# A block with an MLP by Strassen: sums on VectorE, two weight sums kept in DRAM, four products in sequence

## The chip, the core and the metric

The program runs on one core of a Trainium2 chip. Times are device microseconds. The kernel before was timed three times: 778.31, 778.51 and 778.95 us. The change is timed against it on the same chip, and beside it stands one profiled execution of each kernel.

The core has a matrix engine (TensorE, PE in the profile, with its weight loads shown as PEld), VectorE (DVE), ScalarE (ACT), GpSimd (POOL) and SyncE (SP). SyncE issues most of the loads here; GpSimd's and ScalarE's queues issue some DMAs too. Each engine takes its own instructions in a fixed order and waits on semaphores for the others.

## The reference

One encoder block on 512 tokens of width 1024: two attention branches with gates, a norm, and then the part that is changed, a gated MLP and its norm.

```python
u, g = jnp.split(x @ w_ffn_in[layer], 2, axis=-1)          # 1024 -> 2 x 2816
h = jax.nn.gelu(causal_dwconv(u, conv_w[layer], conv_b[layer])) * g
x = layer_norm(DEEPNORM_ALPHA * x + h @ w_ffn_out[layer], ln2_g[layer], ln2_b[layer])
```

All is float32. The kernel writes each operand of a product as a high part in a shorter format (float32r) and a low part, and forms a product from three matmuls: high by high, high by low, low by high.

## The kernel before, in words

**The MLP's first product** runs over 22 blocks of 128 features (the index f). Each needs a piece of weights u_f and a piece g_f, and each piece feeds 24 matmuls over 8 chunks of 128 rows (function ffn_in, lines 701 to 707). `activate(f)` (from line 712) does the causal convolution, the GELU and the product with g: ScalarE copies u out of PSUM (L715), VectorE does three steps (L717 to L719), ScalarE the GELU (L720), VectorE the multiplication into `hp` (L724), which also frees g's PSUM bank.

**The MLP's second product** takes the features two blocks at a time: a pair i holds an even and an odd block, 11 pairs in all (NP). Tokens fall into two halves of 256, output columns into two halves of 512. On this two-by-two scheme Strassen's method needs seven products m1 to m7 where eight would be plain. Each of the seven costs, for one pair, 2 blocks of 128 tokens by 3 matmuls.

Three of the seven (m3, m4 and the part of m1 for that pair) are done inside the first stage, one pair after another (`second_half`, 18 matmuls a pair). Their weights come as two pieces p_i of 512 KB, which `mix_weights` (L752 to L754) turns into sums on GpSimd. Their activations come from `sides` (L726 to L747), which forms sums and differences of the four quarters of `hp` on GpSimd (L735, L738 to L740) and splits them on ScalarE and VectorE. `gh`, `gl` are used at once; `eh`, `el` are kept for all 11 pairs.

The other four products (m5, m7 added into m1, m2, and m6 added into m3; 66 matmuls each) form the second stage. Their weights are loaded again as 22 pieces: a_i holds both feature halves of the right output columns, b_i of the left ones; one GpSimd sum per piece (`mix_low` L760, `mix_top` L767), then the split. A piece a_i serves m5 and m7, b_i serves m2 and m6. The last five b pieces are held in SBUF (HELD), so that block 0 can be finished first, and then block 1: m2, then m6 in two halves of 256 columns.

**Loads and splits.** The class `Stream` (lines 53 to 111) has one list of pieces in order. When a piece is asked for (`get`), loads and splits are issued up to three pieces ahead. A raw piece lands in one of three buffers `raw` (in the second stage two more, `raw2`, for some pieces); ScalarE writes the high part (L94), VectorE the low part (L96; GpSimd for some early pieces), into a ring of three slots `whi`, `wlo` or where `place` names another home. A slot is free when the matmuls of its last piece are done. SyncE issues the loads in the order of the list and waits at each for its raw buffer.

**Order and memory.** The program is traced in the order of the code; a planner with a model of the engines' times then sets the order on each engine, and the semaphores follow. `tc.issue_after(x)` puts the instructions of its block behind x on their engine. The PSUM banks are two pools of four: `pa` holds m4, then m5 and m2, beside the u and g in work; `pb` holds m3 and m1, later the last half of m6. When the first stage is over its tiles are given up and the pool `wp` takes their place.

**The end.** `into` (L859 to L866) adds a product into the residual row tiles x1[j] on VectorE, `finish(j)` (L868 to L884) normalises a tile of 128 tokens and writes it out. Tiles 0 and 1 are finished while m2 and m6 run, tile 2 during block 1, tile 3 after the last matmul.

Of the kernel before, what the change touches and what calls it, by code (L numbers as in the profile page):

```python
# [24 lines left out]
NP = FC // 2  # L25
# [13 lines left out]
HELD = 5  # L39
# [13 lines left out]
class Stream:  # L53


    def __init__(self, nc, raw, ring, pieces, ahead_load, ahead_split, place=None, lo_on_pool=()):
# [5 lines left out]
        self.mixed, self.homes = {}, {}  # L62
        self.nl = self.ns = 0

    def _advance(self, upto):
        nc = self.nc
        n = len(self.pieces)
        while self.nl < min(n, upto + self.al):
            key, src = self.pieces[self.nl]
            srcs = src if isinstance(src, tuple) else (src,)  # L70
            ts = []
            for m, one in enumerate(srcs):
                t = self.home(key, m)
                w = int(np.prod(one.shape[1:]))
                dst = t[:, :w]
                nc.sync.dma_start(dst if len(one.shape) == 2 else dst.rearrange("p (a b) -> p a b", b=one.shape[-1]), one)
                ts.append(t)
            self.loaded[self.nl] = (ts, w)
            self.nl += 1
        while self.ns < min(n, upto + self.asp, self.nl):  # L80
            ts, w = self.loaded.pop(self.ns)
            key = self.pieces[self.ns][0]
            if key in self.mixed:
                parts = self.mixed[key](ts)
            else:
                parts = [(ts[0], w, key)]
            out = ()
            for t, w, where in parts:
                if where in self.place:
                    hi, lo = self.place[where](where)  # L90
                else:
                    hi = self.ring.tile([128, 1024], F32R, tag="whi", name=f"whi_{self.ns}")
                    lo = self.ring.tile([128, 1024], F32R, tag="wlo", name=f"wlo_{self.ns}")
# [5 lines left out]
            self.ns += 1  # L99

# [14 lines left out]
def tile_block(ctx: ExitStack, tc: tile.TileContext, xT, xN, w_qi, w_ki, w_t, w_v, w_br, w_o, w_fi, w_fo,  # L115
# [52 lines left out]
    low, top = ([(f"{key}{i}", w_fo[:, i, :, b * 512:b * 512 + 512].rearrange("d p n -> p d n")) for i in range(NP)]  # L168
                for b, key in ((1, "a"), (0, "b")))
# [7 lines left out]
    st = Stream(nc, rawp, ring, order, 3, 3, place, POOL_LO)  # L177

# [547 lines left out]
    def sides():  # L726
# [3 lines left out]
        sm = tp.tile([128, 5, HT], F32, tag="sm", bufs=1, name=f"sm{i}")  # L730
        gh = tp.tile([128, 3, HT], F32R, tag="gh", bufs=1, name=f"gh{i}")
        gl = tp.tile([128, 3, HT], F32R, tag="gl", bufs=1, name=f"gl{i}")
        nc.scalar.activation(gh[:, 0:2], hp[:, 1:3], AF.Copy)
        nc.vector.tensor_sub(gl[:, 0:2], hp[:, 1:3], r32(gh[:, 0:2]))
        nc.gpsimd.tensor_add(sm[:, 4], hp[:, 1], hp[:, 2])  # L735
        nc.scalar.activation(gh[:, 2], sm[:, 4], AF.Copy)
        nc.vector.tensor_sub(gl[:, 2], sm[:, 4], r32(gh[:, 2]))
        nc.gpsimd.tensor_add(sm[:, 0:2], hp[:, 0:2], hp[:, 2:4])  # L738
# [4 lines left out]
        nc.scalar.activation(a, sm[:, 0:4], AF.Copy)  # L743
        nc.vector.tensor_sub(b, sm[:, 0:4], r32(a))
# [3 lines left out]

    def mix_weights(ts):
# [3 lines left out]
        nc.gpsimd.tensor_sub(a[:, 1], a[:, 1], a[:, 0])  # L753
        nc.gpsimd.tensor_add(a[:, 0], a[:, 0], b[:, 1])  # L754
        return [(ts[1], 512, "pb"), (ts[0], 1024, "pa")]

    def mix_low(key):
        def f(ts):
            w = ts[0].rearrange("p (d n) -> p d n", d=2)
            nc.gpsimd.tensor_add(w[:, 0], w[:, 0], w[:, 1])  # L760
            return [(ts[0], 1024, key)]
        return f

    def mix_top(key):
        def f(ts):
            w = ts[0].rearrange("p (d n) -> p d n", d=2)
            nc.gpsimd.tensor_add(w[:, 1], w[:, 0], w[:, 1])  # L767
            return [(ts[0], 1024, key)]
# [5 lines left out]

    place["pb"] = place_low
    for i in range(NP):
        st.mixed[f"p{i}"] = mix_weights
        st.mixed[f"a{i}"] = mix_low(f"a{i}")
        st.mixed[f"b{i}"] = mix_top(f"b{i}")
# [27 lines left out]
    for f in range(FC):  # L807
        if f == 0:
            ups, gps_ = ps0[0], ps0[1]
        else:  # L810
# [5 lines left out]
            if f % 2 == 0:  # L816
# [3 lines left out]
                second_half(f // 2 - 1, h, st.get(f"p{f//2-1}"))  # L820
            gps_ = pa("g_ps")
# [6 lines left out]
    wa = []  # L828

    def fifth(i, blocks=(0, 1)):  # L830
        product(m5, (eh[i][:, 1], el[i][:, 1]), [w[:, second_c] for w in wa[i]], i == 0, i == NP - 1, blocks)

    def seventh(i):
        product(m1, (eh[i][:, 2], el[i][:, 2]), [w[:, first_c] for w in wa[i]], False, i == NP - 1)

    last = st.get(f"p{NP-1}")
    wa.append(st.get("a0"))
    fifth(0)
# [4 lines left out]
    def place_b(key):  # L843
        return (wp.tile([128, 1024], F32R, tag="dh", bufs=HELD, name=f"{key}h"),
                wp.tile([128, 1024], F32R, tag="dl", bufs=HELD, name=f"{key}l"))

    for key in ["a2", "a3", "a4"] + [f"b{i}" for i in range(NP - HELD, NP)]:
        place[key] = place_b

    def more_raw(key):  # L850
        return wp.tile([128, 1024], F32, tag="raw2", bufs=2, name=f"raw_{key}")

    for n, key in enumerate([f"a{i}" for i in range(2, NP)] + [f"b{i}" for i in range(NP)]):
        if n % 5 in (1, 3):
            st.homes[key, 0] = more_raw
# [31 lines left out]
    for i in (1, 2):  # L887
        wa.append(st.get(f"a{i}"))
        fifth(i)
    second_half(NP - 1, h, last)  # L890
    wa.append(st.get("a3"))
    fifth(3)
    for t in range(2):
        into(2 + t, second_c, m1[t], 1.0, first=True)
    for i in range(4):
# [129 lines left out]
```

## Time and profile before

| | us |
|---|---|
| median of three runs | 778.51 |
| the profiled execution | 783.59 |
| its span, first to last instruction | 781.8 |
| TensorE busy in it | 756.8 (97%) |
| VectorE busy | 561.6 (72%) |
| ScalarE busy | 355.9 (46%) |
| GpSimd busy | 251.2 (32%) |

The MLP's first product runs from about 414 us to 697.6, the second stage of the second product from there to 772.6, the last norm and output to 781.8. A group's row names line, engine, operation, output<-inputs, shapes and count, then busy us and mean ns, then the idle time before and who ended it. A row of waits gives total us, times and the longest. A row by stretch gives its length, then busy time and number of instructions of each engine, TensorE's granted clock (1.00 is full), the DMA engines' busy share and GB/s. A timeline row gives start and duration. Matmuls overlap in the pipeline: 0.39 us is the way through, and the step from one to the next is shorter.

### The profile page before, as it was taken

To read this page: it belongs to the slowest core of one execution; us is meant where nothing else is said; L and a number is where in the kernel's file an instruction comes from. 1 tells how busy PE (TensorE), PEld (TensorE's weight loads), DVE (VectorE), ACT (ScalarE), POOL (GpSimd) and SP (SyncE) were. 2 spreads that over 40 slices of the span, in tenths; PEclk is the share of its full clock that TensorE was granted. 3 is DMA by queue.
4 is the path that set the end of the run, shared out by engine and by line. 5 is a ranking of instruction groups with operands and counts; after the bars stand their busy time and mean duration, and the time that the engine had idled before them with its cause. 6 is when DMAs were issued, how large, how long until landed. Compare 5 with 4: busy or idle time off the path is not lost.

```text
span 781.8 us, 9787 instructions
## 1 busy us (share of the span) xinstructions
PE 756.8 (97%) x3579; PEld 630.7 (81%) x3579; DVE 561.6 (72%) x826; ACT 355.9 (46%) x550; POOL 251.2 (32%) x227
## 2 busy tenths in 40 slices
PE   8999999999999999999999999999999999988985
PEld 6788887788888888888889888888888888877864
DVE  5579999977666575658663766776676667776797
ACT  5546654656564746836211533433344334433340
POOL 2002534527814110000100442334233423466451
PEclk9999999999999999999999999999999999999998
DMA  7642332233324333126700443333334332438532
GB/s 241 222 157 81 108 108 68 68 109 83 106 95 121 95 106 97 54 81 224 288 0 1 135 137 130 109 133 122 126 107 135 132 120 98 132 111 257 174 119 97
DMA packets 32160, 95.55 MB, mean 122 GB/s; under 512 B 3880, under 2 KB 4280, under 8 KB 32112
## 3 DMA queue, kind: packets, MB, share of 16 engines
q1 hardware_dynamic: 27728, 84.19, 33.1%
q10 hardware_dynamic: 2576, 6.29, 3.0%
q0 software_dynamic: 1808, 4.44, 1.6%
q8 instruction: 28, 0.46, 0.2%
q14 instruction: 20, 0.16, 0.1%
HBM read 88.59 MB, written 4.21 MB: 119 GB/s over the span
## 4 chain that ended last, share of the span: by engine, by line
PE 68%; DVE 7%; issue 3%; POOL 2%; ACT 1%; DMA 1%; POOLq 0%; DVEq 0%; ACTq 0%
PE u_ps L706 5%; PE u_ps L707 5%; PE g_ps L706 5%; PE g_ps L707 5%; PE g_ps L705 5%; PE u_ps L705 5%; PE m_ps L786 3%; PE m_ps L787 3%; PE m_ps L788 3%; PE av_ps L404 2%; PE ga_ps L254 2%; PE ga_ps L253 2%; PE ga_ps L255 2%; PE o_ps L665 2%; PE o_ps L664 2%
## 5 line engine op out<-in xcount | busy, mean ns | idle before, releaser
L96 DVE TENSOR_TENSOR wlo<-raw,whi 128x1024 fp32r<-128x1024 f32 (+2 forms) x104 | 146.1, 1406 | 70.9 <-ACT whi L94 67.8
L94 ACT ACTIVATE whi<-raw 128x1024 fp32r<-128x1024 f32 (+2 forms) x123 | 126.2, 1027 | 110.7 <-issue 35.0
L705 PE MATMUL u_ps<-x1h,whi 128*128 128x512 f32 (+1 forms) x192 | 71.5, 373 | 0.2 <-ACT x1h L688 0.2
L706 PE MATMUL u_ps<-x1l,whi 128*128 128x512 f32 (+1 forms) x192 | 71.4, 372 | 0.1
L707 PE MATMUL u_ps<-x1h,wlo 128*128 128x512 f32 (+1 forms) x192 | 71.3, 372 | 0.0
L706 PE MATMUL g_ps<-x1l,whi 128*128 128x512 f32 (+1 forms) x184 | 69.9, 380 | 0.0
L705 PE MATMUL g_ps<-x1h,whi 128*128 128x512 f32 (+1 forms) x184 | 69.9, 380 | 0.0
L707 PE MATMUL g_ps<-x1h,wlo 128*128 128x512 f32 (+1 forms) x184 | 69.9, 380 | 0.0
L96 POOL TENSOR_TENSOR wlo<-raw,whi 128x1024 fp32r<-128x1024 f32 x19 | 46.2, 2435 | 18.6 <-ACT whi L94 18.5
L720 ACT ACTIVATE c<-c,cwt 128x512 f32<-128x512 f32 x22 | 15.9, 724 | 59.7 <-DVE c L719 59.7
L705 PEld LDWEIGHTS u_ps<-x1h,whi 128*128 128x128 f32 x192 | 36.2, 188 | 6.8 <-ACT x1h L688 0.5
L706 PEld LDWEIGHTS u_ps<-x1l,whi 128*128 128x128 f32 x192 | 36.2, 188 | 6.5 <-DVE x1l L689 0.3
L707 PEld LDWEIGHTS u_ps<-x1h,wlo 128*128 128x128 f32 x192 | 36.2, 188 | 6.2
L705 PEld LDWEIGHTS g_ps<-x1h,whi 128*128 128x128 f32 x184 | 34.6, 188 | 6.6
L707 PEld LDWEIGHTS g_ps<-x1h,wlo 128*128 128x128 f32 x184 | 34.6, 188 | 6.5
L706 PEld LDWEIGHTS g_ps<-x1l,whi 128*128 128x128 f32 x184 | 34.6, 188 | 6.5
L393 DVE TENSOR_TENSOR ptl<-tr_ps,pth 128x512 fp32r<-128x512 f32 (+1 forms) x48 | 27.4, 595 | 13.6 <-ACT pth L392 13.5
L445 POOL TENSOR_TENSOR beta<-beta,keep 128x1280 f32<-128x1280 f32 x8 | 20.6, 2570 | 48.6 <-DVE keep L444 43.2
L714 POOL MEMSET u<- 128x2 f32 x22 | 2.1, 99 | 89.5 <-DVE c L719 89.5
L622 POOL DMA_DIRECT2D ln<-in_lnp_dram x4 | 2.3, 573 | 82.6 <-PE ga_ps L255 82.6
L392 ACT ACTIVATE pth<-tr_ps 128x512 fp32r<-128x512 f32 (+1 forms) x48 | 23.5, 520 | 11.3 <-PE tr_ps L388 8.9
L724 DVE TENSOR_TENSOR hp<-g_ps,c 128x512 f32<-128x512 f32 x22 | 15.2, 690 | 18.1 <-PE g_ps L707 16.5
(563 smaller groups left out, 2095.9 us busy)
## 6 DMA issues: line engine op xcount, KB each, us to landing
raw<-in_w_fi_dram SPq DMA_DIRECT2D x44, 512.0 KB, 3.3
raw<-in_w_fo_dram SPq DMA_DIRECT2D x37, 512.0 KB, 3.4
raw<-in_w_t_dram SPq DMA_DIRECT2D x32, 512.0 KB, 3.4
raw<-in_w_v_dram SPq DMA_DIRECT2D x8, 512.0 KB, 4.3
raw<-in_w_br_dram SPq DMA_DIRECT2D x8, 512.0 KB, 3.3
raw<-in_w_o_dram SPq DMA_DIRECT2D x8, 512.0 KB, 4.1
xr<-in_xT_dram SPq DMA_DIRECT2D x8, 256.0 KB, 5.0
raw<-in_w_qi_dram SPq DMA_DIRECT2D x8, 256.0 KB, 4.2
```

The lines of the kernel that those rows point to most:

```text
L94: nc.scalar.activation(hi[:, :w], t[:, :w], AF.Copy)
L96: self.low = eng.tensor_sub(lo[:, :w], t[:, :w], r32(hi[:, :w])).ins
L392: nc.scalar.activation(th[:, :width], ps[:, :width], AF.Copy)
L393: lows = nc.vector.tensor_sub(tl[:, :width], ps[:, :width], r32(th[:, :width]))
L445: nc.gpsimd.tensor_mul(beta, beta, keep[:, 1:ATT + 1])
L705: nc.tensor.matmul(ps[:, c], wh[:, kc], x1h[:, k, c], start=(k == 0), stop=False)
L706: nc.tensor.matmul(ps[:, c], wh[:, kc], x1l[:, k, c], start=False, stop=False)
L707: nc.tensor.matmul(ps[:, c], wl[:, kc], x1h[:, k, c], start=False, stop=(k == KC - 1))
L720: nc.scalar.activation(c, c, AF.Gelu_apprx_tanh, bias=cwt[:, f, 3:4])
L786: nc.tensor.matmul(o, xh_[:, r], wh[:, c], start=start, stop=False, skip_group_check=True)
L787: nc.tensor.matmul(o, xh_[:, r], wl[:, c], start=False, stop=False, skip_group_check=True)
L788: mm = nc.tensor.matmul(o, xl_[:, r], wh[:, c], start=False, stop=stop, skip_group_check=True)
```

## The change

- **Sums on VectorE.** All sums of `sides` and `mix_weights` go from GpSimd to VectorE. Some are made in place in `hp`; the two sums that keep a tile of their own have one buffer `sm` between them. `eh`, `el` are split in two parts (three quarters, one quarter). p_i's second raw piece gets a buffer of its own (`rawb`).
- **Two weight sums kept.** After p_i a new piece s_i, without a load, calls `keep_sums`: from the mixed weights it forms the weights of m6 (split at once into high and low part) and of m7 (kept whole, float32) on VectorE and ScalarE, and GpSimd's queue writes the three 256 KB tiles to DRAM.
- **Four products in sequence.** The second stage's weights come in units of two pairs: v (six loads, raw right quarter, for m5), x (m7's sum from DRAM, split on chip), y (raw left quarter, m2), z (m6's high and low part from DRAM, straight to their place, no split). The order is m5, then the last pair's `second_half`, then m7, m2, m6. The buffers `raw2` and HELD are gone; six buffers of 8 KB per partition take the units that are not in the ring.
- **Order around it.** m5's first two units run block 0 and then block 1. The additions into x1 move to where their products end. g2 and b2 are loaded after m5. z's loads stand behind y's on SyncE's queue. m6's whole second block is done in halves of 256 columns.

```diff
+            if key in self.direct:
+                ts = self.tiles(key)
+                for t, one in zip(ts, src):
+                    w = int(np.prod(one.shape[1:]))
+                    nc.sync.dma_start(r32(t[:, :w]).rearrange("p (a b) -> p a b", b=512), one)
...
-            order.append((f"p{f//2-1}", (w_fo[0, f // 2 - 1], w_fo[1, f // 2 - 1])))
+            order += [(f"p{f//2-1}", (w_fo[0, f // 2 - 1], w_fo[1, f // 2 - 1])), (f"s{f//2-1}", ())]
...
-    order += low + top
+    order += raw_half("v", 1, slice(512, 1024))
+    order += [(f"x{u}", sums[u][2].rearrange("i p n -> p i n")) for u in range(NU)] + raw_half("y", 0, slice(0, 512))
+    kept = [(f"z{u}", [sums[u][n].rearrange("i p n -> p i n") for n in range(2)]) for u in range(NU)]
...
-        nc.gpsimd.tensor_add(sm[:, 4], hp[:, 1], hp[:, 2])
...
-        nc.gpsimd.tensor_add(sm[:, 0:2], hp[:, 0:2], hp[:, 2:4])
-        nc.gpsimd.tensor_sub(sm[:, 2], hp[:, 3], hp[:, 2])
-        nc.gpsimd.tensor_sub(sm[:, 3], hp[:, 0], hp[:, 1])
+        nc.vector.tensor_add(s1, hp[:, 1], hp[:, 2])
...
+        nc.vector.tensor_sub(s3, hp[:, 0], hp[:, 1])
+        nc.vector.tensor_add(hp[:, 0:2], hp[:, 0:2], hp[:, 2:4])
+        nc.vector.tensor_sub(hp[:, 2], hp[:, 3], hp[:, 2])
...
-        nc.gpsimd.tensor_sub(b[:, 0], b[:, 0], b[:, 1])
-        nc.gpsimd.tensor_sub(a[:, 1], a[:, 1], a[:, 0])
-        nc.gpsimd.tensor_add(a[:, 0], a[:, 0], b[:, 1])
+        nc.vector.tensor_sub(b[:, 0], b[:, 0], b[:, 1])
+        nc.vector.tensor_sub(a[:, 1], a[:, 1], a[:, 0])
+        nc.vector.tensor_add(a[:, 0], a[:, 0], b[:, 1])
...
+    def keep_sums(i):
+        def f(_):
+            a, b = (t.rearrange("p (k n) -> p k n", k=2) for t in mixing[i])
+            nc.vector.tensor_add(b[:, 0], b[:, 0], a[:, 0])
+            whole_ = tp.tile([128, 512], F32, tag="s7", bufs=1, name=f"s7_{i}")
+            nc.vector.tensor_add(whole_, a[:, 1], a[:, 0])
+            hi = tp.tile([128, 512], F32R, tag="sh", bufs=1, name=f"sh{i}")
+            lo = tp.tile([128, 512], F32R, tag="sl", bufs=1, name=f"sl{i}")
+            nc.scalar.activation(hi, b[:, 0], AF.Copy)
+            nc.vector.tensor_sub(lo, b[:, 0], r32(hi))
+            for n, half in enumerate((r32(hi), r32(lo), whole_)):
+                nc.gpsimd.dma_start(sums[i // 2][n, i % 2], half)
+            return []
...
+    def unit(pss, row, key, u, w, blocks=(0, 1), c=slice(0, 512), start=True):
+        for n in range(min(2, NP - 2 * u)):
+            i = 2 * u + n
+            part = [x[:, n * 512:n * 512 + 512] for x in w]
+            mm = product(pss, (eh[i][:, row], el[i][:, row]), part, start and i == 0, i == NP - 1, blocks, c)
+        return mm
...
+    v = [st.get("v0"), st.get("v1")]
+    for t in range(2):
+        for u in range(2):
+            unit(m5, 1, "v", u, v[u], (t,))
+    second_half(NP - 1, h, last)
...
+    for u in range(2, NU):
+        w = st.get(f"v{u}")
+        if firsts:
+            with tc.issue_after(st.low):
+                for _ in range(2):
+                    into(*firsts.pop(0), 1.0, first=True)
+        unit(m5, 1, "v", u, w)
+    g2, b2 = bcast(wp, 2), bcast(wp, 3)
+    held = []
+    for u in range(NU):
+        unit(m1, 2, "x", u, st.get(f"x{u}"), start=False)
+        if u == 0:
+            for t in range(2):
+                into(t, second_c, m5[t], 1.0, stats=1)
+                into(t, first_c, m5[t], -1.0)
+    for u in range(NU):
+        unit(m2, 0, "y", u, st.get(f"y{u}"))
+        with tc.issue_after(st.load):
+            held.append(zt.get(f"z{u}"))
+        if u < 2:
+            into(u, first_c, m1[u], 1.0, stats=0)
+            finish(u)
+    for u in range(NU):
+        mm = unit(m3, 3, "z", u, held[u], (0,), start=False)
...
+        for u in range(NU):
+            mm = unit(m3, 3, "z", u, held[u], (1,), lo_c, start=False)
+    into(3, slice(512, 768), m3[1][:, lo_c], 1.0, stats=1)
     with tc.issue_after(mm):
+        for u in range(NU):
+            unit(end, 3, "z", u, held[u], (1,), hi_c, start=True)
```

More of the change, by code (lines that the diff above doesn't have):

```diff
@@ L75, in _advance @@
                 dst = t[:, :w]
-                nc.sync.dma_start(dst if len(one.shape) == 2 else dst.rearrange("p (a b) -> p a b", b=one.shape[-1]), one)
+                self.load = nc.sync.dma_start(dst if len(one.shape) == 2 else dst.rearrange("p (a b) -> p a b", b=one.shape[-1]), one).ins
                 ts.append(t)
-            self.loaded[self.nl] = (ts, w)
+            self.loaded[self.nl] = (ts, w if ts else 0)
             self.nl += 1
@@ L88, in _advance @@
             for t, w, where in parts:
[L89 to L93, printed above, removed]
+                hi, lo = self.tiles(where)
                 nc.scalar.activation(hi[:, :w], t[:, :w], AF.Copy)
@@ L99, in _advance, with tiles @@
             self.ns += 1
+    def tiles(self, key):
+        if key in self.place:
+            return self.place[key](key)
+        return tuple(self.ring.tile([128, 1024], F32R, tag=f"w{n}", name=f"w{n}_{key}") for n in ("hi", "lo"))
     def home(self, key, m):
@@ L167, in tile_block @@
     order += [(f"wo{k}", w_o[k]) for k in range(KC)]
-    low, top = ([(f"{key}{i}", w_fo[:, i, :, b * 512:b * 512 + 512].rearrange("d p n -> p d n")) for i in range(NP)]
-                for b, key in ((1, "a"), (0, "b")))
+    sums = [nc.dram_tensor(f"s_sum{u}", (3, min(2, NP - 2 * u), 128, 512), F32, kind="Internal").ap() for u in range(NU)]
     for f in range(FC + 1):
@@ L841, in tile_block, with place_unit @@
     wc, wp = open_pool("wp", side="right", reuse_waits="tile")
[L843 to L855, printed above, removed]
+    def place_unit(key):
+        t = wp.tile([128, 2048], F32R, tag="d", bufs=6, name=f"d_{key}")
+        return t[:, :1024], t[:, 1024:]
+    for key in (f"{k}{u}" for k in "vxyz" for u in range(NU)):
+        if key not in RING_UNITS:
+            place[key] = place_unit
     parts2 = [padded(dp, [128, 3 if j == 3 else 2, 6], name=f"parts2_{j}") for j in range(NB)]
@@ L902, in tile_block @@
         if firsts:
             with tc.issue_after(st.low):
-                into(*firsts.pop(0), 1.0, first=True)
-        fifth(i)
-        seventh(i)
-    m2 = [pa(f"m2_ps{t}") for t in range(2)]
-    def second(i, w, blocks):
-        return product(m2, (eh[i][:, 0], el[i][:, 0]), [x[:, first_c] for x in w], i == 0, i == NP - 1, blocks)
-    def sixth(i, w, blocks, c=slice(0, 512), pss=m3, start=False):
-        return product(pss, (eh[i][:, 3], el[i][:, 3]), [x[:, second_c] for x in w], start, i == NP - 1, blocks, c)
@@ L916, in tile_block @@
-    for i in range(2):
-        w = st.get(f"b{i}")
-        second(i, w, (0, 1))
-        sixth(i, w, (0, 1))
-    for t in range(2):
-        into(t, second_c, m5[t], 1.0, stats=1)
-        into(t, first_c, m5[t], -1.0)
-        into(t, first_c, m1[t], 1.0, stats=0)
-    for i in range(2, NP - HELD):
-        w = st.get(f"b{i}")
-        second(i, w, (0, 1))
-        sixth(i, w, (0, 1))
-    held = [(i, st.get(f"b{i}")) for i in range(NP - HELD, NP)]
-    finish(0)
-    finish(1)
-    for i, w in held:
-        second(i, w, (0,))
-        mm = sixth(i, w, (0,))
@@ new lines, in tile_block @@
+    m2 = [pa(f"m2_ps{t}") for t in range(2)]
+    for u in range(NU):
[7 more added lines that the diff above has]
+        mm = unit(m3, 3, "z", u, held[u], (0,), start=False)
+        if u == 0:
+            for t in range(2):
+                into(2 + t, first_c, m2[t], 1.0, stats=0)
+                into(2 + t, second_c, m2[t], -1.0)
+            into(3, slice(768, 1024), m3[1][:, 256:512], 1.0)
@@ L940, in tile_block @@
     with tc.issue_after(mm):
-        for i, w in held:
-            mm = second(i, w, (1,))
+        for u in range(NU):
+            mm = unit(m3, 3, "z", u, held[u], (1,), lo_c, start=False)
+    into(3, slice(512, 768), m3[1][:, lo_c], 1.0, stats=1)
     with tc.issue_after(mm):
-        for i, w in held:
-            mm = sixth(i, w, (1,), lo_c)
-    into(3, first_c, m2[1], 1.0, stats=0)
-    into(3, second_c, m2[1], -1.0)
-    into(3, second_c, m3[1], 1.0)
-    nc.vector.bn_stats(parts2[3][:, 1], x1[3][:, 512:768])
-    with tc.issue_after(mm):
-        for i, w in held:
-            sixth(i, w, (1,), hi_c, end, i == NP - HELD)
+        for u in range(NU):
+            unit(end, 3, "z", u, held[u], (1,), hi_c, start=True)
     into(3, slice(768, 1024), end[1][:, hi_c], 1.0, stats=2)
```

69 lines of the change are left out of this document (29 added, 40 removed).

## The prediction

> **What bounds the kernel now.** I read the page first, then busy time by stretch, then what TensorE waits for, then the last 10 us. The page's head:
>
> ```profile
> span 781.8 us, 9787 instructions
> PE 756.8 (97%) x3579; PEld 630.7 (81%) x3579; DVE 561.6 (72%) x826; ACT 355.9 (46%) x550; POOL 251.2 (32%) x227
> ```
>
> TensorE is the bound, so a change that keeps the number of matmuls can only win time in which TensorE stands still. By stretch (busy us, instructions, clock, share of the DMA engines, GB/s):
>
> ```profile
> core 0: us, PE busy (x) PEld busy (x) DVE busy (x) ACT busy (x) POOL busy (x), PEclk, DMA share, GB/s
> 500.00:600.00 100.00, 100.00 (x443) 82.84 (x442) 69.41 (x65) 38.59 (x50) 35.49 (x36) 1.00 0.39 127
> 697.50:772.70 75.20, 67.81 (x299) 54.31 (x297) 62.22 (x72) 24.23 (x25) 37.06 (x27) 0.98 0.50 161
> 697.50:716.36 18.86, 14.60 (x56) 11.09 (x55) 14.64 (x14) 7.71 (x9) 10.95 (x10) 0.91 0.65 209
> 716.36:746.05 29.69, 29.69 (x132) 24.59 (x131) 21.19 (x24) 10.06 (x10) 15.76 (x11) 1.00 0.58 182
> 746.05:772.70 26.65, 23.52 (x113) 18.63 (x111) 26.38 (x36) 6.47 (x7) 10.35 (x7) 1.00 0.32 103
> ```
>
> In the first stage TensorE never stops: 443 matmuls in 100 us, **0.226 us each**. Nothing can be won there, only lost. The second stage, from the last g matmul to the last matmul, is another matter. By the code it holds 18 + 4 x 66 = 282 products of 512 columns, 15 of them cut into 30 halves. The cost of a half is in the tail's rows (start, duration):
>
> ```profile
> 768.87 0.28 PE L786 MATMUL m_ps<-b6h,eh 128*128 128x256 f32 x1
> ...
> 772.34 0.28 PE L788 MATMUL m_end<-b10h,el 128*128 128x256 f32 x1
> ...
> 774.26 0.41 DVE L864 SCALAR_TENSOR_TENSOR r<-m_end,r 128x256 f32<-128x256 f32 x1
> ...
> 777.69 1.45 ACTq L884 DMA_DIRECT2D out_dram<-r  x3
> ```
>
> From the first to the 30th half are 29 steps in 3.47 us, 0.12 us each. The stage needs 267 x 0.226 + 30 x 0.12 = 63.9 us and takes 75.1 (697.58 to 772.62): **11.2 us lost**. And after the last matmul ends (772.62) VectorE comes to the end product only at 774.26, 1.64 us later, being still at older work. What TensorE waited for in the second stage:
>
> ```profile
> PE m_ps L786 <- DVE hp L724: 2.3, 1, 2.3
> PE m_ps L786 <- DVE r L862: 2.0, 1, 2.0
> PE m_ps L787 <- DVE b9l L96: 2.0, 1, 2.0
> PE m_ps L787 <- DVE wlo L96: 0.8, 1, 0.8
> ```
>
> Every wait is for VectorE. It is slow there because GpSimd runs beside it:
>
> ```profile
> L96 DVE TENSOR_TENSOR wlo<-raw,whi 128x1024 fp32r<-128x1024 f32 x48 | 76.4, 1592 | 24.7 <-ACT whi L94 24.7
> L96 DVE TENSOR_TENSOR a4l<-raw,a4h 128x1024 fp32r<-128x1024 f32 x1 | 1.2, 1212 | 0.0
> L734 DVE TENSOR_TENSOR gl<-hp,gh 128x512 fp32r<-128x512 f32 x9 | 16.0, 1777 | 0.0
> L601 DVE TENSOR_TENSOR ml<-ga,mh 128x512 fp32r<-128x512 f32 x8 | 5.4, 683 | 0.7 <-ACT mh L600 0.7
> L738 POOL TENSOR_TENSOR sm<-hp 128x512 f32<-128x512 f32 x10 | 22.2, 2222 | 0.0
> L753 POOL TENSOR_TENSOR raw<-raw 128x512 f32<-128x512 f32 x10 | 13.8, 1377 | 12.5 <-DMA raw<-in_w_fo_dram 12.5
> ```
>
> The same low-part subtraction takes 1.21 us alone and 1.59 on the mean; 128x512 takes 0.68 (L601) and, beside L738, 1.78.
>
> **The change, part by part.** *First stage: sums move to VectorE.* One pair of feature blocks is 96 + 18 = 114 matmuls, 25.7 us, of which VectorE is busy 69.4% = 17.8. Uncontended, after the change: five 1024-wide subtractions 5 x 1.21, one 512-wide 0.68; the conv and gate chain twice, taken as 4 x 0.69 us (near L601's row; c's other steps are of that size); three weight sums and the three new instructions of keep_sums 6 x 0.68; the sides 3 x 0.68 + 4 x 0.41 + 0.95, with 0.41 from the 256-wide L864 above. Sum 6.7 + 5.5 + 4.1 + 4.6 = 20.9 us, 81%. It fits, and g's PSUM bank (freed by L724) is wanted only after the next u, 24 x 0.226 = 5.4 us after g ends; that covers some misordering. ScalarE gains about 0.9 us a pair on 38.59%. I take **0**; the upper bound is the durations staying contended (x1.59/1.21 = 27.5 us), 1.8 us for each of ten pairs, 18 us. A lower bound below zero is excluded: TensorE is full.
>
> *The DRAM copies.* 33 writes of 256 KB on GpSimd's queue, 0.79 MB per 25.7 us, 31 GB/s on top of 127. They wait for the low part; queued behind them is only the next u's memset, so L717 could be late, again under the 5.4 us. Units x and z read them 20 us or more later. 0.
>
> *Start of the second stage.* m5 used to run 3 matmuls on block 0 and then needed g's bank:
>
> ```profile
> 693.84 2.29 DVE L96 TENSOR_TENSOR wlo<-raw,whi 128x1024 fp32r<-128x1024 f32 x1 [2.97 <-ACT whi L94]
> 696.05 1.51 DVE L717 TENSOR_SCALAR c<-u,cwt 128x512 f32<-128x512 f32 x1
> ...
> 699.93 0.69 DVE L724 TENSOR_TENSOR hp<-g_ps,c 128x512 f32<-128x512 f32 x1 [0.79 <-ACT c L720]
> ```
>
> L96 at 1.21 instead of 2.29 and L717 without its 1 us of blocking bring L724 to about 698. Now block 0 has 12 matmuls (2.7 us, to 700.3), so that wait goes. What is late next is v1: its ring slot is g21's, free at 697.6, then ScalarE 1.05 and VectorE 1.21 bring its low part to about 700.2, against 698.9 + two high products. I take **1.0** (0 to 2.3, today's wait).
>
> *v2.* The splits run three pieces ahead of the one asked for, so v2, v3 and v4 are split before the new six-buffer area is named and go to the ring. v2's slot is that of p10, which the last eighteen products read to their end. ScalarE already stands there today:
>
> ```profile
> ACT whi L94 <- PE m_ps L788: 17.0, 8, 4.3
> L94 ACT ACTIVATE whi<-raw 128x1024 fp32r<-128x1024 f32 x48 | 50.6, 1054 | 31.8 <-issue 21.2 <-POOL raw L754 6.2 <-PE g_ps L706 3.0
> ```
>
> TensorE's only other work, m1 with x0, comes later in its order, so it stops for 1.05 + 0.25 of semaphores = **1.3** (1.1 if the handover is quick; 3.6 if two reads of m1 at 0.68 and the low part at 1.21 go first). The wait on m1 (2.0 us today) itself goes: v2 to v5, 9.5 us, lie between.
>
> *The clock after a stop.* After today's stop at 707 the clock fell:
>
> ```profile
> 706.00:708.00 2.00, 1.18 (x6) 0.64 (x4) 1.09 (x1) 1.60 (x2) 1.83 (x2) 1.00 0.98 360
> 708.00:710.00 2.00, 0.81 (x4) 0.68 (x5) 2.00 (x4) 1.27 (x2) 1.99 (x4) 1.00 0.79 230
> 710.00:712.00 2.00, 2.00 (x7) 1.61 (x6) 2.00 (x1) 0.00 (x0) 1.08 (x1) 0.63 0.92 317
> 712.00:714.00 2.00, 2.00 (x6) 1.53 (x5) 1.31 (x2) 0.40 (x1) 0.00 (x0) 0.51 0.46 113
> ```
>
> 2 x (0.37 + 0.49) = 1.7 us lost, behind 2 us of idleness; the equally long stops at 698 and 760 cost no clock. I take half, **0.8** (0 to 1.7). The Trainium skill, "TensorE: Matmul & The Clock Gate", section "HAM oscillation — how this bites in real kernels", asks only that no idle gap exceed about 3.4 us; by it the term would be 0 and the sum 0.8 us less. The rows show a drop after a shorter stop, so I keep the half.
>
> *v, x, y with three raw buffers in place of five.* A buffer is held for landing, split and handover:
>
> ```profile
> raw<-in_w_fo_dram SPq DMA_DIRECT2D x37, 512.0 KB, 3.4
> ...
> ln<-in_lnp_dram POOLq DMA_DIRECT2D x4, 512.0 KB, 6.6
> raw_a<-in_w_fo_dram SPq DMA_DIRECT2D x3, 512.0 KB, 5.3
> ```
>
> 3.4 + 1.05 + 1.21 + about 1 = 6.7 us, over 3 = 2.2 us per unit, against 12 x 0.226 = 2.7 us that TensorE spends on it. GpSimd's sum (L760, L767) no longer stands in this chain. Narrow but enough: **0.5** (0; at 5.3 and contended 1.59, 9 us / 3 = 3.0, 0.3 short on 15 units: 4.5). The two ln loads, moved on GpSimd's queue to behind v5, run beside x's loads; their rows are wanted by the first norm, 15 us later, against 6.6 to land.
>
> *z loaded ready-made.* No split, but 1 MB a unit on SP's queue, where y4 and y5 now stand behind z0 and z1. From y3's load on, the queue must bring y3 to y5 and z, 7.1 MB, beside 1.0 MB of output. y3 goes when y0's buffer is free, about 10.7 us into x (x0 to x2 8.1, then the split 2.5); z5 is wanted 15 + 15 + 5 x 1.36 = 36.6 us into x. That leaves 25.9 us, less 2 to land. The rows of 0.98 share above move 360 GB/s; q1 over the page moved
>
> ```profile
> q1 hardware_dynamic: 27728, 84.19, 33.1%
> ```
>
> 84.19 MB in 258.8 us, 325 GB/s: 8.1 MB in 24.9 us. **1.0** late (0 at 360; 4.2 at 288 GB/s, the fullest of the page's 40 slices):
>
> ```profile
> GB/s 241 222 157 81 108 108 68 68 109 83 106 95 121 95 106 97 54 81 224 288 0 1 135 137 130 109 133 122 126 107 135 132 120 98 132 111 257 174 119 97
> ```
>
> *Matmuls and tail.* Block 1 of z is now 66 halves in place of 33: 249 x 0.226 + 66 x 0.12 = 64.2 us. VectorE has nothing else at the end (m3's upper half and m2 are added before), so the tail is 0.2 + (781.8 - 774.26) = 7.7 us, not 9.2 (0 to 1.5 better).
>
> **Sum:** 697.6 + 64.2 + (1.0 + 1.3 + 0.8 + 0.5 + 1.0 = 4.6) + 7.7 = 774.1, 7.7 us under the span of 781.8. The profiled execution took 783.59 us, 1.8 around its span and 5.1 over the median; I take the difference off the median: 778.5 - 7.7 = **770.8 us**.
>
> **Rivals.** *All hidden*: scheduling covers v1, v2 and z, no drop of the clock: only 1.1 is left of 4.6: 767.3. For: 132 matmuls in 29.69 us without a gap. Against: v2's slot.
>
> *VectorE binds* (first stage contended as now, or three raw buffers short): a quarter of the 18 us, or 4.5 for the buffers where I took 0.5, gives 774.8 to 775.3. For: 81% leaves 5 us a pair, and VectorE itself now stands in front of w_fo's loads, for which GpSimd waited 12.5 us (L753). Against: with p's right half in a buffer of its own the loads go out earlier.
>
> *The stops only move*: v1 2.3, v2 3.6, clock 1.7, buffers 2, z 2, 11.6 in all: 777.8, within the measurement of before. About 0.2% (1.6 us) is what a measurement of this kernel tells from no change. For: VectorE's order is planned ahead, and each of these waits hangs on it.
>
> *Slower: z comes late.* If the queue keeps only the 209 GB/s of 697.50:716.36, 8.1 MB take 38.8 us, z5 is 14.9 late instead of 1.0: 770.8 + 13.9 = 784.7. It decides below 8.1 MB in 33.5 us, 240 GB/s. Against: that stretch was waiting for buffers, at 0.65 share.
>
> **How the numbers follow.** Forecast 0.57, all hidden 0.13, VectorE binds 0.15, stops move 0.07, z late 0.08. The range runs from 766.5 to 777.5 and leaves out z late, most of "stops move" and the tail of the rest, about 0.18; the forecast's own range is 768.5 to 773.5. Faster: 0.57 + 0.13 + 0.15 less a little, 0.84; same 0.07; slower 0.09.
>
> **What would show it.** Right: low-part subtractions near 1.21 us throughout; the first stage full at 443 matmuls per 100 us; TensorE's second stage 66 to 70 us; a stop of 1 to 2 us where v2's high part comes; the tail under 8 us. Wrong: L724 late and TensorE waiting for it within the first stage; L786 waiting for z's load; a second stage over 73 us.

## The result, and the profile after

The changed kernel takes **772.91 us** (median of seven, 772.49 to 775.81), the kernel before 778.95 beside it (seven, 777.95 to 781.07). The ratio is **0.9927, 95% interval 0.9908 to 0.9946**: 5.7 us faster (4.2 to 7.2). The profiled execution took 773.86 us, its span is 771.7.

The page's head of the changed kernel, and its busy time by stretch (columns as in the prediction):

```profile
span 771.7 us, 9924 instructions
PE 753.8 (98%) x3597; PEld 630.3 (82%) x3597; DVE 563.6 (73%) x944; ACT 358.4 (46%) x568; POOL 136.3 (18%) x161
```

```profile
500.00:600.00 100.00, 100.00 (x443) 82.84 (x442) 73.98 (x108) 41.88 (x59) 7.24 (x20) 1.00 0.45 153
695.80:762.70 66.90, 65.39 (x316) 54.37 (x314) 48.80 (x73) 18.60 (x21) 3.98 (x5) 1.00 0.64 224
734.00:750.00 16.00, 15.63 (x70) 12.61 (x69) 11.82 (x21) 2.75 (x3) 1.98 (x2) 1.00 1.05 392
```

The first stage is as full as before: 443 matmuls in 100 us, with VectorE at 74% instead of 69%. The second stage is 66.9 us instead of 75.1, and the clock stays at 1.00. New is the last row: for 16 us the DMA engines are full.

What TensorE still waits for in the second stage (total us, times, longest):

```profile
PE m_ps L818 <- DMA d_z<-s_sum: 1.1, 1, 1.1
PE m_ps L817 <- DMA d_z<-s_sum: 0.4, 1, 0.4
```

All four waits for VectorE are gone; only z's loads are left. Counted by steps between matmuls, these waits with the slow start behind each cost 2.3 us, and 0.2 us goes at a low part of y. The stage needs 64.2 us, so 2.7 us are lost where 11.2 were (the last 0.2 comes from rounding the step of one matmul).

Its start and end in the timeline (start, duration):

```profile
695.80 0.39 PE L817 MATMUL m_ps<-whi_v,eh 128*128 128x512 f32 x1
...
762.42 0.28 PE L819 MATMUL m_end<-d_z,el 128*128 128x256 f32 x1
762.73 0.42 DVE L894 SCALAR_TENSOR_TENSOR r<-m_end,r 128x256 f32<-128x256 f32 x1 [2.61 <-PE m_end L819]
...
766.18 1.45 ACTq L914 DMA_DIRECT2D out_dram<-r  x3
```

VectorE comes to the end product 0.03 us after the last matmul, not 1.64. From there to the end of the span it is 9.0 us where it was 7.5.

### The profile page after: what moved, and what is told of

It reads as the page before. It is cut to its first block, busy times and chain, and to the rows that moved or that the text cites. A ratio compares the mean times of both kernels' runs of the same rounds, so it can differ in the third digit from the quotient of the medians.

```text
span 771.7 us, 9924 instructions
## 1 busy us (share of the span) xinstructions
PE 753.8 (98%) x3597; PEld 630.3 (82%) x3597; DVE 563.6 (73%) x944; ACT 358.4 (46%) x568; POOL 136.3 (18%) x161
## 4 chain that ended last, share of the span: by engine, by line
PE 75%; DMA 3%; DVE 2%; issue 0%; ACT 0%; POOL 0%; POOLq 0%; ACTq 0%
PE u_ps L728 5%; PE u_ps L729 5%; PE g_ps L729 5%; PE g_ps L728 5%; PE g_ps L727 5%; PE u_ps L727 5%; PE m_ps L818 4%; PE m_ps L819 4%; PE m_ps L817 4%; DMA d_z<-s_sum 3%; PE av_ps L426 2%; PE ga_ps L276 2%; PE ga_ps L277 2%; PE ga_ps L275 2%; PE o_ps L687 2%; PE o_ps L685 2%
## 5 line engine op out<-in xcount | busy, mean ns | idle before, releaser
L727 PE MATMUL u_ps<-x1h,whi_u 128*128 128x512 f32 (+1 forms) x192 | 71.5, 372 | 0.3 <-ACT x1h L710 0.3
L728 PE MATMUL u_ps<-x1l,whi_u 128*128 128x512 f32 (+1 forms) x192 | 71.4, 372 | 0.1
L729 PE MATMUL u_ps<-x1h,wlo_u 128*128 128x512 f32 (+1 forms) x192 | 71.3, 372 | 0.0
L727 PE MATMUL g_ps<-x1h,whi_g 128*128 128x512 f32 (+1 forms) x184 | 69.9, 380 | 0.0
L729 PE MATMUL g_ps<-x1h,wlo_g 128*128 128x512 f32 (+1 forms) x184 | 69.9, 380 | 0.0
L728 PE MATMUL g_ps<-x1l,whi_g 128*128 128x512 f32 (+1 forms) x184 | 69.9, 380 | 0.0
L727 PEld LDWEIGHTS u_ps<-x1h,whi_u 128*128 128x128 f32 x192 | 36.2, 188 | 6.7 <-ACT x1h L710 0.5
L728 PEld LDWEIGHTS u_ps<-x1l,whi_u 128*128 128x128 f32 x192 | 36.2, 188 | 6.5 <-DVE x1l L711 0.3
L729 PEld LDWEIGHTS u_ps<-x1h,wlo_u 128*128 128x128 f32 x192 | 36.2, 188 | 6.3
L729 PEld LDWEIGHTS g_ps<-x1h,wlo_g 128*128 128x128 f32 x184 | 34.6, 188 | 6.6
```

What stands on the lines that cost most here:

```text
L727: nc.tensor.matmul(ps[:, c], wh[:, kc], x1h[:, k, c], start=(k == 0), stop=False)
L728: nc.tensor.matmul(ps[:, c], wh[:, kc], x1l[:, k, c], start=False, stop=False)
L729: nc.tensor.matmul(ps[:, c], wl[:, kc], x1h[:, k, c], start=False, stop=(k == KC - 1))
```

## The experiments

Each is timed against the kernel before on the same chip; ratios are to that, with 95% intervals. The chips differ from one experiment to the next, so runs are best compared by their ratios.

### The kernel before once more

No edit. 

> The kernel before, unchanged, profiled once more. My sum started from a profiled execution of 783.59 us, 4.6 above the median of 778.95. Theory 1: that execution lost more in the second stage than the usual one; a new profile then shows a span of 776 to 779 and a second stage (last g matmul to last matmul) of 71 to 73 us in place of 75.1. Theory 2: the second stage always takes 75 us and the excess lies elsewhere (the first 40 us, the end); then the stage shows 74.5 to 75.5 again.

Measured: 778.73 us, ratio 0.9991 (0.9975 to 1.0008). Its profile has a span of 776.5, 5.3 us shorter than the one on which the prediction rests. The waits in the second stage:

```profile
PE m_ps L786 <- DVE hp L724: 2.0, 1, 2.0
PE m_ps L787 <- DVE b9l L96: 1.9, 1, 1.9
PE m_ps L786 <- DVE r L862: 0.8, 1, 0.8
PE m_ps L787 <- DVE wlo L96: 0.6, 1, 0.6
```

The same four, but L862 costs 0.8 instead of 2.0 and no drop of the clock follows. The stage runs from 696.00 to 767.33, 71.3 us, with 7.4 lost. The end product is again 1.62 us late (767.33 to 768.95). So the first profile caught an execution of this kernel that is not typical of it (783.59 us; the seven timed beside the change lie between 777.95 and 781.07). Between this second profile and that of the changed kernel the spans differ by 4.8 us, and the parts add up to it: 0.2 for the earlier start of the stage, 4.4 in the stage, 1.6 at the end product, less 1.4 behind it.

### All sums of the kernel before on VectorE

```diff
-        nc.gpsimd.tensor_add(sm[:, 4], hp[:, 1], hp[:, 2])
+        nc.vector.tensor_add(sm[:, 4], hp[:, 1], hp[:, 2])
...
-            nc.gpsimd.tensor_add(w[:, 0], w[:, 0], w[:, 1])
+            nc.vector.tensor_add(w[:, 0], w[:, 0], w[:, 1])
```

and likewise the other sums of `sides`, `mix_weights`, `mix_low` and `mix_top`. 

> The kernel before with all its weight and activation sums on VectorE instead of GpSimd, nothing else of the change (a and b pieces, no copies in DRAM, the old order). Theory 1 (the contended subtractions made the stops): the 128x1024 low parts fall from 1.59 to 1.21-1.25 us, TensorE's stops in the second stage halve, 775 to 777 us. Theory 2 (the new order and the missing sums of the second stage matter, not the engine): VectorE gets 22 sums of 0.68 us more in the second stage, in line with the splits, and gains nothing: 778 to 781 us.

Measured: 781.96 us, ratio 1.0027 (1.0014 to 1.0041), **slower** by 2.1 us (1.1 to 3.2). The profile's waits in the second stage, the longest of TensorE and one of VectorE, and two stretches of it:

```profile
PE m_ps L787 <- DVE b8l L96: 2.8, 1, 2.8
PE m_ps L786 <- ACT whi L94: 1.6, 1, 1.6
DVE raw L760 <- DMA raw<-in_w_fo_dram: 7.7, 5, 2.8
```

```profile
700.00:702.00 2.00, 2.00 (x7) 1.52 (x6) 2.00 (x5) 0.64 (x3) 0.00 (x0) 0.50 0.69 234
758.00:760.00 2.00, 2.00 (x5) 1.61 (x6) 2.00 (x3) 0.00 (x0) 0.00 (x0) 0.50 0.00 0
```

No low part is stretched here (1.22 us each), but the 22 sums now take VectorE's own time in the stage where it is the late engine, and VectorE also stands idle for the loads in front of five of them (7.7 us). TensorE's waits add up to 6.0 us, little more than the 5.3 in the second profile of the kernel before. What is new is the clock: it drops at two of the stops, and the slower matmuls there cost about 1.6 us each time. So in this execution the loss is in good part the clock. Moving all sums to VectorE, with nothing else of the change, loses.

### The changed kernel with its first-stage sums back on GpSimd

```diff
-        nc.vector.tensor_add(s1, hp[:, 1], hp[:, 2])
+        nc.gpsimd.tensor_add(s1, hp[:, 1], hp[:, 2])
...
-        nc.vector.tensor_sub(b[:, 0], b[:, 0], b[:, 1])
+        nc.gpsimd.tensor_sub(b[:, 0], b[:, 0], b[:, 1])
```

and the other sums of `sides` and `mix_weights`; the sums of `keep_sums` stay on VectorE. 

> The changed kernel with the sums of sides and mix_weights back on GpSimd (the two sums of keep_sums stay on VectorE); DRAM copies and the new order stay. Theory 1: the low parts in the first stage go back to 1.4-1.6 us, the last pair's chain is late again and TensorE stops 1 to 3 us at the start of the second stage: 774 to 776 us. Theory 2 (the order alone carries the gain): 772.5 to 773.5, no stop for L746 or L756.

Measured: 772.4 us, ratio 0.9907 (0.9884 to 0.9930), no different from the changed kernel. The low parts of the first stage are longer again:

```profile
L105 DVE TENSOR_TENSOR wlo_g<-raw,whi_g 128x1024 fp32r<-128x1024 f32 x19 | 26.9, 1417 | 3.5 <-ACT whi_g L103 3.5
```

against 1.22 us in the changed kernel (the row is quoted in the section on the steps). That costs nothing that this run can tell: the first stage has room. So the engine of the first-stage sums, the first part of the change, is not where the gain comes from.

### The kernel before without its second-stage sums

```diff
-            nc.gpsimd.tensor_add(w[:, 0], w[:, 0], w[:, 1])
...
-            nc.gpsimd.tensor_add(w[:, 1], w[:, 0], w[:, 1])
```

The products then use the second half of each pair unsummed; loads, splits and matmuls stay. 

> The kernel before, with the 22 sums that GpSimd makes of the second stage's weights left out (the products then use the unsummed second half of each pair, so the output is not the reference's); order, transfers, splits and matmuls stay. Theory 3: the stops of the second stage that the traces of before put down to low parts (wlo 0.8, b9l 2.1, b10l 0.3 us in its second profile) come from the chain transfer, GpSimd sum, split, low part, which is one step longer than in the changed kernel; without the sum they go and the time is 774 to 776 us, a span of 773 or so against 776.5. Rival (order): the low parts are late because VectorE's queue holds the additions of finished products and the first two blocks' norms ahead of them; then the sums matter little and the time stays 777.5 to 779.

Measured: 773.4 us, ratio 0.9912 (0.9883 to 0.9941), 6.9 us less than the kernel before. TensorE's waits in the second stage:

```profile
PE m_ps L784 <- DVE r L860: 0.7, 1, 0.7
PE m_ps L784 <- DVE hp L724: 0.2, 1, 0.2
```

So without these 22 sums, and with nothing else changed, the kernel gains as much as the change does (4.6 to 9.1 us, against 4.2 to 7.2). The second stage loses 2.1 us (66.0 taken, 63.9 needed); the end product is still 1.65 us late, in the old order of products.

### The same sums made, but not used

```diff
-            nc.gpsimd.tensor_add(w[:, 0], w[:, 0], w[:, 1])
+            nc.gpsimd.tensor_add(aside(), w[:, 0], w[:, 1])
```

and the same in `mix_top`. The sums cost GpSimd the same, but the split no longer waits for them. 

> The kernel before, in which GpSimd still makes the second stage's 22 sums from the same raw halves, but writes them to a tile that nothing reads (the products use the unsummed half, so the output is not the reference's). The split no longer waits for the sum, and the sum still runs beside VectorE's work. If it is the extra step in the chain transfer, sum, split, low part that makes the stops, the time is that of the run without the sums, 773 to 774.5 us. If it is that VectorE's instructions are longer while GpSimd adds (low parts of 1.46 to 2.38 us in the second profile of before, 1.21 to 1.28 without the sums), the low parts stay long and the time stays 777 to 779.5. In between, 775 to 776.5, both count.

Measured: 777.51 us, ratio 0.9979 (0.9961 to 0.9997). Of the 6.9 us only 1.6 (0.3 to 3.0) come back when the sum leaves the chain; the other 5.3 hang on whether GpSimd adds while VectorE works. The intervals of the two runs don't overlap. VectorE's groups in the second stage, first without the sums, then with the sums set aside:

```profile
L96 DVE TENSOR_TENSOR wlo<-raw,whi 128x1024 fp32r<-128x1024 f32 x10 | 12.7, 1275 | 6.0 <-ACT whi L94 6.0
L96 DVE TENSOR_TENSOR a4l<-raw,a4h 128x1024 fp32r<-128x1024 f32 x1 | 1.2, 1218 | 0.0
```

```profile
L96 DVE TENSOR_TENSOR wlo<-raw,whi 128x1024 fp32r<-128x1024 f32 x10 | 14.6, 1459 | 5.3 <-ACT whi L94 5.3
L96 DVE TENSOR_TENSOR a4l<-raw,a4h 128x1024 fp32r<-128x1024 f32 x1 | 2.4, 2372 | 0.0
```

The same instruction on the same data takes 1.22 us or 2.37. The Trainium skill, "SBUF — State Buffer", section "SBUF: two separate sides", says that a VectorE instruction with two SBUF inputs and a GpSimd instruction that reads SBUF exclude each other for the whole of the one that came first. These rows agree: a low part that meets a sum is longer by 1.15 us, close to a sum's length (L753's 1.38 us in the prediction).

TensorE's two longest waits with the sums set aside (this execution took 775.95 us, 1.6 under the run's median, so its waits are rather short), and the instruction in VectorE's line before each that is longer than without the sums:

```profile
PE m_ps L789 <- DVE hp L724: 1.6, 1, 1.6
PE m_ps L790 <- DVE b9l L96: 1.2, 1, 1.2
```

```profile
693.85 1.80 DVE L719 SCALAR_TENSOR_TENSOR c<-u,cwt,c 128x512 f32<-128x512 f32 x1
...
748.55 1.78 DVE L635 SCALAR_TENSOR_TENSOR r<-r,mv,ln 128x512 f32<-128x512 f32 x1
```

Without the sums L719 takes 0.75 us there and L635 0.74. L719 stands ahead of the multiplication L724, L635 ahead of the low part b9l. So VectorE is late because its instructions are longer while GpSimd adds.

### z's loads four units earlier

```diff
+        if u >= 2:
+            with tc.issue_after(st.load):
+                held.append(zt.get(f"z{u-2}"))
...
-        with tc.issue_after(st.load):
-            held.append(zt.get(f"z{u}"))
...
+            with tc.issue_after(st.load):
+                held.append(zt.get(f"z{u+4}"))
```

The first lines stand in the loop over x, the last in that over y under `u < 2`. 

> The changed kernel with each z unit asked for four units earlier (z0 to z3 beside x2 to x5, z4 and z5 beside y0 and y1), nothing else. Theory 1 (the 2.2 us that TensorE still loses are the DMA engines at 1.05 share and 392 GB/s between 734 and 750 us, where y, z and output come together): the loads spread, no matmul waits for d_z, 770.7 to 771.7 us. Theory 2 (z only changes places with x and y, which have three raw buffers): waits for splits of x or y appear instead, 772.5 to 775 us.

Measured: 779.13 us, ratio 0.9990 (0.9976 to 1.0005): the whole gain is gone. No matmul waits for z's loads, but one waits elsewhere:

```profile
PE m_ps L817 <- DVE r L894: 4.2, 1, 4.2
PE m_ps L818 <- DVE wlo_y L105: 0.8, 1, 0.8
```

and the clock is halved there (the columns of the stretches):

```profile
757.00:759.00 2.00, 0.61 (x3) 0.61 (x4) 1.97 (x5) 0.00 (x0) 0.00 (x0) 0.50 0.00 0
```

With its weights there early, the planner put all 33 matmuls of z's block 0 ahead of y's last (14 in the changed kernel), so none of them was left to cover VectorE's additions of m2. Block 1 of z needs m3's upper half read first, and that addition, at 757.93, stood behind five other additions and two rows of statistics that VectorE began at 753.74.

### The same with that addition moved up

```diff
                 into(t, first_c, m5[t], -1.0)
+            into(3, slice(768, 1024), m3[1][:, 256:512], 1.0)
```

taken from its place in the loop over z. 

> The changed kernel with the transfers of the last product's weights issued four units earlier, as in the run before, and with the addition of the upper half of the second block's third product moved from the last product's start to the start of the seventh product, right behind the additions of the fifth. Theory: the 4.2 us stop and the half clock behind it in the run before came from that one addition standing behind four others in VectorE's queue, so with both edits neither the wait for the transfer (about 2.0 us lost in the changed kernel) nor that stop is left: 770.3 to 771.5 us, ratio to the kernel before 0.989 to 0.991. Rival: the bank itself is read late by VectorE whatever the order in the text, or another addition takes the place of this one: 773 to 779.

Measured: 777.29 us, ratio 0.9963 (0.9947 to 0.9978) where 0.989 to 0.991 was forecast, a miss by 4 to 6 us. In its profile (775.84 us, 1.5 under the run's median; span 774.1) the 4.2 us stop is gone and the last matmul ends at 761.7, 1.0 us before the changed kernel's. But VectorE is still at the third block:

```profile
762.42 0.41 DVE L894 SCALAR_TENSOR_TENSOR r<-m_end,r 128x256 f32<-128x256 f32 x1
...
763.53 1.41 DVE L657 SCALAR_TENSOR_TENSOR r<-r,mv,ln 128x512 f32<-128x512 f32 x2
...
765.71 1.00 ACTq L904 DMA_DIRECT2D out_dram<-r  x2
...
768.50 1.45 ACTq L914 DMA_DIRECT2D out_dram<-r  x3
```

The norm of block 2 (L657), finished at 759 us in the changed kernel, now runs behind the end product, and the last tile's outputs go from 768.50 on instead of 766.18.

### The order held back

```diff
-    for u in range(NU):
-        mm = unit(m3, 3, "z", u, held[u], (0,), start=False)
+    with tc.issue_after(mm):
+        for u in range(NU):
+            mm = unit(m3, 3, "z", u, held[u], (0,), start=False)
```

on top of the last two edits; `mm` is y's last matmul. 

> The run with early transfers and the early addition, with the last product's first block held back until the second product is through, as the text has it, so that VectorE's four additions of the second product are covered by that block's 7.4 us. Theory: the time before was lost at the end, where VectorE's additions and the norm of the third block stood ahead of the last block's (last addition 0.8 us late, last output 2.3 us later than in the changed kernel); with the order held both the waits for the transfers (2.0 us) and this go: 770.5 to 771.5. Rival: without the last product's matmuls between them the second product waits for its own split weights, whose transfers now stand behind the others: 772.5 to 776.

Measured: 780.81 us, ratio 1.0014 (0.9998 to 1.0030): another miss. TensorE now waits for y:

```profile
PE m_ps L818 <- DVE wlo_y L105: 4.4, 4, 3.0
PE m_ps L817 <- ACT whi_y L103: 2.1, 3, 1.5
```

```profile
732.00:748.00 16.00, 12.44 (x45) 9.25 (x46) 11.40 (x19) 3.48 (x4) 1.98 (x2) 0.89 1.03 383
```

With the DMA engines full (share 1.03), y's raw pieces come later: the second and third of them took 9.6 and 11.4 us to land, in the changed kernel 5.0 and 5.4. The 3.0 us stop drops the clock as well.

### The writes on SyncE's queue

```diff
-                nc.gpsimd.dma_start(sums[i // 2][n, i % 2], half)
+                nc.sync.dma_start(sums[i // 2][n, i % 2], half)
```

> The changed kernel with the 33 writes of the sums issued from SyncE's queue in place of GpSimd's. Theory 4: the 3.0 us between the last output byte and the end of the span, against 1.6 to 1.7 us in kernels without these writes, is paid for the GpSimd queue's DMAs; it falls to about 1.6 us and the time to 771.0 to 771.9. Rival a: the longer end is due to the added DRAM buffers or to something else of the program, and stays 3.0 us: 772.5 to 773.3. Rival b: SyncE's queue waits at each write for the sum, the weights behind it arrive late, and TensorE stops in the first stage: over 774.

Measured: 773.79 us (five runs, 771.57 to 775.46), ratio 0.9920 (0.9893 to 0.9947). In its profile (span 769.4) the last tile's outputs are issued from

```profile
765.39 1.45 ACTq L914 DMA_DIRECT2D out_dram<-r  x3
```

on, 4.0 us before the end of the span; in the changed kernel it is 766.18 and 771.7, 5.5. The mechanism shows, the gain in time does not: the interval holds both 1.5 us and nothing.

The same edit on the held-back order, timed beside it on one chip: 

> The same with the 33 writes of the sums on SyncE's queue. The 1.5 us shorter end (4.0 us from the issue of the last output to the end of the span, against 5.5 in the changed kernel) should come on top: 769.0 to 770.2, ratio to before 0.987 to 0.989. If the spread of the other runs with these writes on that queue (771.6 to 775.5) is its price, it is 771 to 774 and no better than the changed kernel.

Measured: 778.10 us, ratio 0.9981 (0.9967 to 0.9996), 2.7 us under its twin's 780.81, with 5.5 us from the last tile's outputs to the end in the twin and 4.0 here. The forecast of 769 to 770 was a miss with the held-back order itself, but in this pair the time is lower too; the shorter end explains 1.5 of the 2.7 us.

### Two units earlier, with the writes on SyncE

```diff
+        if u >= 4:
+            with tc.issue_after(st.load):
+                held.append(zt.get(f"z{u-4}"))
...
+        if u < 4:
+            with tc.issue_after(st.load):
+                held.append(zt.get(f"z{u+2}"))
```

The first lines stand in the loop over x, the last in that over y; with it go the early addition and the writes on SyncE, and the order is the planner's own. 

> The changed kernel with the transfers of the last product's weights issued two units earlier (not four), the addition of the upper half of the second block's third product behind the fifth product's, and the 33 writes of the sums on SyncE's queue; the order of the last product's first block is left to the planner. Theory: the transfers from the end of the seventh product on fill the DMA engines (share 1.03 to 1.05, 377 to 392 GB/s from 732 to 748 us in every variant), so they have to be spread into the stretch from 716 to 732 (share 0.56), but not so early that the second product's raw halves stand behind them (the 3.0 us stop of the held-back order) or that VectorE's additions and the third block's norm slide to the end (the run with four units). Then the 2.0 us of waits fall below 1 and the end is 1.5 us shorter: 770 to 771.5. Rival: the bytes are the bound and the wait only changes its place: 772.5 to 775.

Measured: 777.38 us, ratio 0.9971 (0.9956 to 0.9986), outside the forecast and above the rival's 772.5 to 775 too. As the rival said, the wait only changed its place:

```profile
PE m_ps L817 <- ACT whi_y L103: 2.7, 1, 2.7
```

```profile
732.00:748.00 16.00, 14.94 (x61) 10.79 (x60) 11.54 (x19) 3.18 (x3) 1.98 (x2) 1.00 1.05 391
...
750.00:752.00 2.00, 1.26 (x3) 0.83 (x3) 1.27 (x2) 1.21 (x2) 0.00 (x0) 0.55 0.78 300
```

This stop is not a late load, though. The raw piece of y4 that TensorE waits for was issued at 734.77 and took 9.8 us, so it was there at 744.5; ScalarE split it at 749.64:

```profile
740.56 1.06 ACT L103 ACTIVATE whi_y<-raw 128x1024 fp32r<-128x1024 f32 x1 [2.99 <-DMA raw<-in_w_fo_dram]
741.97 7.54 ACTq L904 DMA_DIRECT2D out_dram<-r  x4
749.64 1.57 ACT L103 ACTIVATE whi_y<-raw 128x1024 fp32r<-128x1024 f32 x2 [8.02 <-DMA d_z<-s_sum]
```

Between the two splits ScalarE's line holds the issues of four outputs (L904), which take until 749.5. The last three of them each went 0.07 us after an earlier load had landed (743.18, 745.88 and 749.10, the last is y5's): in the trace each of these loads had used the semaphore that the output takes next. So full DMA engines delay y here by way of the outputs that stand in front of its split. No run issues the outputs from another queue. Of the five orders tried, the changed kernel's, which lets z wait and loses 2.3 us, has the shortest time.

### The additions of m2's second block moved back

```diff
-            for t in range(2):
-                into(2 + t, first_c, m2[t], 1.0, stats=0)
-                into(2 + t, second_c, m2[t], -1.0)
-            into(3, slice(768, 1024), m3[1][:, 256:512], 1.0)
+            into(2, first_c, m2[0], 1.0, stats=0)
+            into(2, second_c, m2[0], -1.0)
...
-    into(3, slice(512, 768), m3[1][:, lo_c], 1.0, stats=1)
+    into(3, first_c, m2[1], 1.0, stats=0)
+    into(3, second_c, m2[1], -1.0)
+    into(3, second_c, m3[1], 1.0)
+    nc.vector.bn_stats(parts2[3][:, 1], x1[3][:, 512:768])
```

> The changed kernel with the additions of the second block of the second product and the upper half of its third product moved back to where the kernel before has them, behind the last product's second block. Theory 5: the last addition then starts late behind them in VectorE's queue, as in the kernel before (1.6 us after the last matmul): 774.0 to 774.8, 1.2 to 1.8 above the changed kernel. Rival: the additions fit beside the last quarter of the matmuls and nothing is late: 772.5 to 773.3.

Measured: 773.39 us, ratio 0.9917 (0.9885 to 0.9948), like the changed kernel. It decides less than was meant: the planner put m2's additions back where their product ends, and only the addition of m3's upper half moved. So this run doesn't say what late additions of m2 would cost. All five profiles in the old order of products come to the end product 1.62 to 2.47 us late, with sums or without; of the nine in the new order, eight come to it within 0.1 us and one (z's loads four units earlier, with the addition moved up) 0.75 us late. That it is the order of the products is thus supported, not isolated.

## Why the prediction was right, and where its steps were not

The time, 772.91 where 770.8 was forecast, lies in the forecast's own range. In what it lost the kernel stands between the forecast and its rival *All hidden*: v1, v2 and the clock cost nothing, as that rival had it, and only z was late. The steps:

**First stage 0: right.** 443 matmuls in 100 us, as before. VectorE is at 74%, not 81%: the durations add up to 79 us in that stretch, but an instruction can start before the one ahead has ended (four additions of 0.68 to 0.69 us start 0.60 us apart from 748.35 on). Its low parts are at the duration the prediction took:

```profile
L105 DVE TENSOR_TENSOR wlo_g<-raw,whi_g 128x1024 fp32r<-128x1024 f32 x22 | 26.8, 1218 | 3.9 <-ACT whi_g L103 3.9
L758 DVE TENSOR_TENSOR gl<-hp,gh 128x512 fp32r<-128x512 f32 x11 | 7.5, 683 | 0.2 <-ACT gh L755 0.2
```

**"Every wait is for VectorE. It is slow there because GpSimd runs beside it": right for the second stage, and shown** by the run with the sums set aside (5.3 of the 6.9 us; 1.6 are the step in the chain). It holds only there: in the first stage the same slowness has no price that the runs can tell, and moving all sums to VectorE, in both stages and with all else as before, loses 2.1 us. What gains is that the second stage has no sums left: they are made in the first, where VectorE has room, and fetched from DRAM. No run has the kept sums in the old order of products, so what the new order is worth by itself is not measured; the run without the sums gains as much in the old one.

**v1 (1.0), v2 (1.3), the clock (0.8): nothing of it came.** The planner ran both blocks of v0 at once, which gave TensorE work until 698.5 and freed v0's ring slot. "v2's slot is that of p10" failed: a slot is taken as it comes free, and ScalarE's split for v2 started with v0's last matmul:

```profile
698.77 1.06 ACT L103 ACTIVATE whi_v<-raw 128x1024 fp32r<-128x1024 f32 x1 [1.03 <-issue]
```

The longest stop was 1.1 us, and the clock stayed at 1.00. **Three raw buffers (0.5): 0.2.**

**z late (1.0): right in kind, 2.3 in size.** The queue moved 392 GB/s over 16 us, more than the 325 taken. But its work began later than the sum had it: y3's load was issued at 728.63, 13.8 us into x and not 10.7, and the last of z landed at 754.02. At the full rate a load took long to land:

```profile
d_z<-s_sum SPq DMA_DIRECT2D x10, 512.0 KB, 9.3
```

Each of the later runs that issued z earlier lost more elsewhere than this wait costs.

**Tail 7.7: 9.0.** VectorE is free at the end as argued, but from the last tile's outputs to the end of the span it is 5.5 us and not 4.1, a term that the sum did not hold. The run with the writes on SyncE's queue shows that it comes with the writes.

In spans: 774.1 was summed, 771.7 came: 1.8 for the earlier start of the stage, 1.9 for the stalls (4.6 to 2.7), less 1.3 for the tail.

**"I take the difference off the median" is the step that failed.** The span of 781.8 belonged to an execution 5.1 us over the median, and the prediction said so, but took all its 11.2 us of stops as this kernel's own. In the second profile they are 7.4. By that one the same terms give 7.4 - 4.6 - 0.3 + 1.5 = 4.0 us of gain, 774.5; the stalls that did not come and the longer end bring it to the 4.8 between the spans. That 770.8 came near is thus in part luck: 3.8 us of stops too many, taken from that one execution, stand against stalls that did not come.

## What to carry to other kernels

When a sum on GpSimd makes VectorE late, ask where VectorE has room, not which engine is free: making the sums in another stage won, moving them to another engine where they stood lost. Before a difference is taken off a profile, look at a second profile of the same kernel: the stops of one execution here were half as long again as those of the next. And before loads are issued earlier, ask what they push back: in the four earlier orders here it was twice VectorE's additions, once the other loads, and once a split on ScalarE that stood behind the issues of outputs.

## What the runs showed of the hardware

**Writes on GpSimd's queue lengthen the program's end.** From the issue of the last tile's outputs to the end of the span it is 5.5 to 5.6 us in all six kernels profiled with the 33 writes on that queue, and 4.0 to 4.2 in those without writes or with them on SyncE's queue. What is done in that time the trace doesn't show.

**The clock drops after stops that differ little from others that leave it alone.** With stops of 2.0 us (before, at 707), 2.7 (two units earlier), 2.8 (all sums on VectorE) and 3.0 (the order held back) came stretches at 0.50 to 0.65, and with two of 1.6 and 1.0 us close together (all sums on VectorE, at 698) one too; stops of 2.3 and 2.0 us in the same profile of before (at 698 and 760) and of 2.0 and 1.9 in its second profile had none. In the traces' record of the clock each of these spells lasts 3.4 us, and 6.8 where the stop was 4.2 us (four units earlier). The Trainium skill's bound of about 3.4 us ("TensorE: Matmul & The Clock Gate", section "HAM oscillation — how this bites in real kernels") is higher than these; what else decides is open.
